# A tuned decoder layer with a product-key expert layer: U blocks, exponential, first loads and LN refinement moved

## The chip, the cores and the metric

The kernel runs on one core of one Trainium2 chip. The metric is the device time of one execution in microseconds (us). A core has five engines that run side by side, each working through its own instructions in order: TensorE (PE; its weight loads are shown apart as PEld), VectorE (DVE), ScalarE (ACT), GpSimd (POOL) and SyncE (SP). SP issues most DMAs, ACT and POOL some. An engine that waits for a semaphore holds up all that stands behind the waiting instruction on it.

## The reference

One inference step of one layer for a prompt of 512 tokens and 8 sequences of 4 tokens, 544 tokens in all, of width 1024. A mixer (pooling and mLSTM, a gated linear recurrence with matrix memory) is followed by PEER, a feed-forward layer that picks 16 of 16384 one-neuron experts for each token and each of 8 heads:

```python
x  = ln(ALPHA * x + (1 + g1) * mixer(ln(x) * (1 + s1) + b1), ln1_g, ln1_b)
u2 = ln(x) * (1 + s2) + b2
q  = (u2 @ w_q).reshape(n, 8, 2, 128)              # two half keys per head
s  = einsum('nhpc,hpkc->nhpk', q, keys)            # scores against 128 sub keys
sv, si = top_k(s, 16)
comb = sv[:, :, 0, :, None] + sv[:, :, 1, None, :]  # 16 x 16 sums
top, sel = top_k(comb, 16); eidx = the experts' numbers (128 * i + j)
g   = softmax(top)
act = gelu(einsum('nd,nhkd->nhk', u2, u_tab[eidx]))
y   = einsum('nhk,nhkd->nd', g * act, v_tab[eidx])
x   = ln(ALPHA * x + (1 + g2) * y, ln2_g, ln2_b)
```

All is float32. u_tab and v_tab have 16384 rows of 1024.

## The kernel before, in words

Float32 products are made from split operands: a weight tile is copied by ACT to a rounded high half (whi, L439), the rest is the low half (wlo, L441, on POOL or DVE), and PE adds three products (high by high, high by low, low by high), 24 matmuls for a 128-row block of w_q or u_tab. The class Weights loads (L414, from SP), splits and hands out these tiles in program order.

**Stages.** Modulation, the first LN, the q, k, v projections and mLSTM come first. Then the out projection: for each of five token tiles (four of 128, one of 32) the LN steps of x1_of run on DVE, POOL and ACT, PE transposes the normalised rows (L160), and u2 and its halves are made. Each LN takes its reciprocal root from ACT and refines it in ln_newton with four DVE instructions of one element per partition (L233 to L239). `halves(0)` is interleaved: the q projection and scores of one half of the tokens.

**halves(1).** The q projection of the other half: 16 steps (hp, head and half key) of 24 matmuls, transposes and scores on PE. ACT copies the scores (L1136), DVE sorts the top 16 (L1102 to L1107) and then the best 16 sums (L1112 to L1116). After the steps listed in PRE, one *U block* (`uphase`, L1174) is put on PE: u_tab rows 128 b to 128 b + 127 against the 384 tokens of the three dense tiles, 24 matmuls into a PSUM bank, then Gelu on ACT (act, L1188); the first SPILL acts are stored to DRAM (Ad, L1190), the last RING stay in SBUF. Every expert of a block is computed for these tokens, so nothing has to be gathered for them.

**Ranks and gates.** `softmax_and_ranks` subtracts the maximum (L1235), takes the exponential on ACT (L1236, with a load of its table, and one for Gelu afterwards), finds each expert's i and j on DVE (L1239 to L1250) and sums and inverts (L1252, L1253). `topk(t)` turns them into numbers and gates g for each tile. The gates of the three dense tiles become a dense array: one-hot masks E (L1318) and P (L1346, E times the gate) on DVE, their products on PE (tile pg, 16 matmuls a group, 24 pairs of two groups), copied by ACT to stage (L1333) and stored to DRAM as Gd in twelve pieces (L1337, ACT's queue).

**The planner.** L1371 to L1392 is a loop at build time with two modelled clocks, pe and dve, the constants GRP, LOU, PEU, PEG, TOFF, LEAD, PEW and a bound GB of groups in flight. It decides whether a DVE step of the side chain (ranks, topk, masks), a pair of gates or a U block comes next. RES blocks are kept for after the last gate; AHEAD = 56 blocks are done before the stream.

**The stream.** From L1588 on, 128 iterations b: a U block (from the iteration on at which todo_u - b is at most RING), then `vprep(b + 2)`, then `ymm(b)`: 18 matmuls (Y) for each of three tiles, coefficients times v rows. vprep (L1476) multiplies act by gate (ar*gr, L1481), splits the loaded v rows (vr; whi on ACT, wlo on DVE) and splits the product (chi on ACT L1484, clo L1485). SP issues the loads: vr (L1459), every fourth time gr from Gd (L1462), and spilled acts ar from Ad (L1470) through the queue object `aq` (class Ahead). The remaining tokens (one prompt tile and the samples) take *gather steps*: POOL gathers rows of u_tab or v_tab by index (L1421), DVE multiplies and sums (L1434 for u, L1446 for v into y); `pace` spreads 320 of them over the iterations. vr and raw share one pool tag of NRAW = 4 buffers.

**The tail.** `finish(t)` per tile: y plus the residual (L1549, L1550), moments (L1558, L1560, L1563), `ln_newton`, scale and shift (ACT L1581, POOL L1582 and L1583), store.

## Time and profile before

| what | value |
|---|---|
| runs, us | 1667.96, 1670.13, 1671.59 (median 1670.13) |
| profiled execution, us | 1665.72, its span 1663.9 |
| busy share of the span | PE 94%, DVE 82%, POOL 43%, ACT 38% |
| mean granted TensorE clock | 0.971 |
| DMA | 455.33 MB, mean 274 GB/s |
| chain that ended last | PE 72%, DVE 16%, DMA 6%, ACT 2%, issue 2% |

The span is the time from the first to the last instruction in the profile; the profiled execution's own time is 1.8 us longer. Stages in it: out projection from about 270 to 423 us, halves(1) to 524, ranks to the first gate at 615, gates to 758, the last U blocks to 787.5, the stream to about 1624, then the tail. Busy time says how long an engine had an instruction running, not whether another waited for it; the waits and the chain say that. The granted clock is a share of TensorE's full clock of 2.4 GHz.

### The profile page before, as it was taken

The numbers are of one execution on the slowest core, as the hardware profiler recorded it, in microseconds if no ns is written. First come the engines' busy times: TensorE is split into PE (matmuls) and PEld (weight loads), VectorE is DVE, ScalarE is ACT, GpSimd is POOL, SyncE is SP. The second block draws the span as 40 slices with busy tenths as digits, with TensorE's granted clock in tenths as the row PEclk, the third lists the DMA queues.
The fourth block names the chain that finished last, engine by engine and source line by source line (L and its number), as shares of the span: only waits on it lengthen the run. The fifth ranks groups of instructions, "written<-read, shape, count | busy, mean of one in ns | idle before, by whom it ended". The sixth has DMA issues, their size and how long they took to land.

```text
span 1663.9 us, 25206 instructions
## 1 busy us (share of the span) xinstructions
PE 1559.0 (94%) x9293; PEld 1386.5 (83%) x9293; DVE 1356.1 (82%) x2734; ACT 632.9 (38%) x999; POOL 712.4 (43%) x521
## 2 busy tenths in 40 slices
PE   5999999896998999999899999999999999999993
PEld 3888777676897999999788889999999999999873
DVE  6634467698996999993688879989999999998986
ACT  4322223445433335554333333333333333333343
POOL 2333333465554000000433336656666666666615
PEclk9999998898999999999899999999999999999997
DMA  8544456443343558876999989999999999999981
GB/s 340 175 145 159 142 148 215 163 165 118 114 142 101 162 163 303 285 274 228 359 364 382 372 297 373 373 371 386 379 372 381 377 371 385 378 369 378 390 281 67
DMA packets 181135, 455.33 MB, mean 274 GB/s; under 512 B 23248, under 2 KB 84304, under 8 KB 179348
## 3 DMA queue, kind: packets, MB, share of 16 engines
q1 hardware_dynamic: 119880, 246.90, 43.3%
q0 software_dynamic: 46080, 167.79, 26.3%
q10 hardware_dynamic: 15052, 39.03, 6.6%
q8 instruction: 73, 1.20, 0.3%
q14 instruction: 50, 0.41, 0.1%
HBM read 412.93 MB, written 40.73 MB: 273 GB/s over the span
## 4 chain that ended last, share of the span: by engine, by line
PE 72%; DVE 16%; DMA 6%; ACT 2%; issue 2%; POOL 1%; SPq 0%; ACTq 0%; DVEq 0%; POOLq 0%
PE pH L156 27%; PE Y L156 25%; PE bk L156 11%; PE tb L156 4%; DMA gr<-Gd 4%; PE pg L156 3%; DVE wlo L441 2%; PE pm L156 1%; DMA wm<-in_w_mod_r_dram 1%; PE tb L160 1%; DVE or L235 1%; DVE y L1446 1%; DVE ost L245 1%; DVE x L979 1%; ACT whi L439 1%
## 5 line engine op out<-in xcount | busy, mean ns | idle before, releaser
L156 PE MATMUL pH<-u2hi,whi 128*128 128x384 f32 x960 | 328.9, 343 | 7.9 <-ACT act L1188 7.9
L156 PE MATMUL pH<-u2hi,wlo 128*128 128x384 f32 x960 | 324.0, 338 | 2.9 <-DVE wlo L441 2.6
L156 PE MATMUL pH<-u2lo,whi 128*128 128x384 f32 x960 | 324.4, 338 | 0.0
L156 PE MATMUL Y<-whi,chi 128*128 128x512 f32 x768 | 301.1, 392 | 8.4 <-ACT chi L1484 8.4
L156 PE MATMUL Y<-whi,clo 128*128 128x512 f32 x768 | 302.6, 394 | 2.2 <-DVE clo L1485 1.5
L1421 POOL DMA_INDIRECT rbuf<-in_v_tab_dram,eid x160 | 237.9, 1487 | 151.8 <-DVE y L1446 104.6
L156 PE MATMUL Y<-wlo,chi 128*128 128x512 f32 x768 | 302.0, 393 | 0.0
L1421 POOL DMA_INDIRECT rbuf<-in_u_tab_dram,eid x160 | 218.4, 1365 | 187.4 <-DVE rbuf L1434 143.2
L439 ACT ACTIVATE whi<-raw 128x1024 fp32r<-128x1024 f32 (+1 forms) x193 | 203.0, 1055 | 200.9 <-issue 126.0
L439 ACT ACTIVATE whi<-vr 128x1024 fp32r<-128x1024 f32 x128 | 135.7, 1060 | 280.6 <-PE Y L156 226.9
L441 POOL TENSOR_TENSOR wlo<-raw,whi 128x1024 fp32r<-128x1024 f32 (+2 forms) x68 | 159.9, 2359 | 181.4 <-ACT whi L439 180.0
L441 DVE TENSOR_TENSOR wlo<-vr,whi 128x1024 fp32r<-128x1024 f32 x128 | 156.5, 1222 | 68.3 <-ACT whi L439 56.7
L1446 DVE SCALAR_TENSOR_TENSOR y<-rbuf,cf,y 128x1024 f32<-128x1024 f32 x158 | 202.6, 1282 | 0.9
L156 PEld LDWEIGHTS pH<-u2hi,whi 128*128 128x128 f32 x960 | 181.0, 189 | 11.2 <-ACT act L1188 8.2
L441 DVE TENSOR_TENSOR wlo<-raw,whi 128x1024 fp32r<-128x1024 f32 (+1 forms) x129 | 155.3, 1207 | 36.9 <-ACT whi L439 34.1
L156 PEld LDWEIGHTS pH<-u2hi,wlo 128*128 128x128 f32 x960 | 180.9, 188 | 5.0 <-DVE wlo L441 4.3
L156 PEld LDWEIGHTS pH<-u2lo,whi 128*128 128x128 f32 x960 | 181.1, 189 | 2.8
L156 PEld LDWEIGHTS Y<-whi,chi 128*128 128x128 f32 x768 | 145.4, 189 | 40.4 <-ACT chi L1484 10.0
L156 PEld LDWEIGHTS Y<-whi,clo 128*128 128x128 f32 x768 | 145.1, 189 | 33.4 <-DVE clo L1485 3.3
L156 PEld LDWEIGHTS Y<-wlo,chi 128*128 128x128 f32 x768 | 145.1, 189 | 30.1
L1434 DVE SCALAR_TENSOR_TENSOR rbuf<-rbuf,utok 128x1024 f32<-128x1024 f32 x128 | 156.1, 1221 | 0.0
L1485 POOL TENSOR_TENSOR clo<-ar,chi 128x384 fp32r<-128x384 f32 x1 | 1.4, 1357 | 250.1 <-DMA ar<-Ad 250.1
(402 smaller groups left out, 2693.5 us busy)
## 6 DMA issues: line engine op xcount, KB each, us to landing
raw<-in_u_b_dram SPq DMA_DIRECT2D x128, 512.0 KB
vr<-in_v_tab_dram SPq DMA_DIRECT2D x128, 512.0 KB
wm<-in_w_mod_r_dram SPq DMA_DIRECT2D x48, 512.0 KB
gr<-Gd SPq DMA_DIRECT2D x32, 768.0 KB
Gd<-stage ACTq DMA_DIRECT2D x9, 2048.0 KB
raw<-in_w_q_b_dram SPq DMA_DIRECT2D x32, 512.0 KB
raw<-in_w_in_b_dram SPq DMA_DIRECT2D x20, 512.0 KB
Ad<-act ACTq DMA_DIRECT2D x43, 192.0 KB
```

What stands on the lines that cost most here:

```text
L156: nc.tensor.matmul(out, l, r, start=start, stop=stop, skip_group_check=True)
L160: nc.tensor.transpose(out, x, idn)
L235: nc.vector.tensor_tensor(r, r, q, op=ALU.mult)
L245: nc.vector.bn_stats(st[:, i, :], x[:, 512 * i:512 * (i + 1)])
L439: nc.scalar.activation(hi, raw, AF.Copy)
L441: e.tensor_tensor(lo[:, d], raw[:, d], f32(hi[:, d]), op=ALU.subtract)
L979: e.tensor_tensor(x1[:, d], x1[:, d], l1b[:rows, d], op=ALU.add)
L1421: nc.gpsimd.indirect_dma_start(out=g, out_offset=None, in_=tab, in_offset=bass.IndirectOffsetOnAxis(ap=eid[t][:, k:k + 1], axis=0))
L1434: nc.vector.scalar_tensor_tensor(g, g, 1.0, u, op0=ALU.mult, op1=ALU.mult, accum_out=dots[:, k:k + 1])
L1446: nc.vector.scalar_tensor_tensor(y2[t], g, cf[:, k:k + 1], y2[t], op0=ALU.mult, op1=ALU.add)
L1485: (nc.vector if b else nc.gpsimd).tensor_tensor(cl, x, f32(ch), op=ALU.subtract)
```

## The change

Constants: PRE has four entries for eight, at steps 4, 7, 10 and 13; AHEAD is 53 for 56, so SPILL 40 for 43; TOFF 10 for 0. ln_newton's three instructions with two tensors become tensor_scalar instructions whose second and third operands are one-element columns read by pointer; the fourth instruction stays. The ranks' function is cut in three: `ranks`, `exps` (issued by the planner's chain after the ranks have been handed out) and `sums` (after the second half of the first topk). The planner's loop ends with the last gate; the blocks left up to AHEAD then stand in a loop of their own, with the loads of spilled acts ahead of them (`aq.fill()`), the first gr when five are left, two gather steps at each of the last three, and vprep(0) and vprep(1) at the last two. WI.early = 2 makes a tile's split go out two calls ahead rather than one, in the planner's loop and until that point.

```diff
-AHEAD = 56
+AHEAD = 53
+GPRE = 2
-TOFF = 0.00
+TOFF = 10.00
-PRE = (6, 8, 10, 11, 12, 13, 14, 15)
+PRE = (4, 7, 10, 13)
...
-        nc.vector.scalar_tensor_tensor(q, r, ve, r, op0=ALU.mult, op1=ALU.mult)
+        nc.vector.tensor_scalar(q, ve, r, r, op0=ALU.mult, op1=ALU.mult)
         nc.vector.tensor_scalar(q, q, -0.5, 1.5, op0=ALU.mult, op1=ALU.add)
-        nc.vector.tensor_tensor(r, r, q, op=ALU.mult)
+        nc.vector.tensor_scalar(r, r, q, None, op0=ALU.mult)
...
-        nc.vector.scalar_tensor_tensor(nm, mv[:, 0:1], sign, r, op0=ALU.mult, op1=ALU.mult)
+        nc.vector.tensor_scalar(nm, mv[:, 0:1], sign, r, op0=ALU.mult, op1=ALU.mult)
...
     def topks():
-        r = softmax_and_ranks()
-        yield 9.0
+        r = ranks()
+        yield 8.5
+        exps(r[0])
...
-            yield 3.7
+            if t == TORD[0] and p:
+                sums(ex, sx)
+            yield 4.2 if K == 128 else 1.6
...
-    while more or wait or b < AHEAD:
+    while more or wait:
...
-        elif b < (AHEAD - RES if more or wait else AHEAD) and not (wait and wait[0][0] <= pe + PEW):
+        elif b < AHEAD - RES and not (wait and wait[0][0] <= pe + PEW):
+            WI.early = 2
...
+    def load_g(b):
+        g = vp.tile([128, 12, 4, 32], F32, name="gr", tag="gr", bufs=2)
+        nc.sync.dma_start(g, Gd[:, :, b:b + 4, :].rearrange("q j i n -> j q i n"))
+        for i in range(4):
+            gpair[b + i] = g
...
-        if b % 4 == 0:
...
+        if b % 4 == 0 and b:
+            load_g(b)
...
-    for b in range(2):
-        vprep(b)
-    todo_u = AHEAD
-    spent, done = 0.0, 0
-    pace = (320 + 1 - GV * (AHEAD - RING) - GV2 * (RING - GEND)) / (NB - AHEAD)
+    todo_u = b
+    aq.fill()
+    while todo_u < AHEAD:
+        if AHEAD - todo_u == 5:
+            load_g(0)
+        if AHEAD - todo_u < 4:
+            steps(gg, GPRE)
+        if AHEAD - todo_u < 3:
+            WI.early = 1
+            vprep(2 - AHEAD + todo_u)
+        uphase(todo_u)
+        todo_u += 1
+    done = 3 * GPRE
+    spent = float(done)
+    pace = (320 + 1 - done - GV * (AHEAD - RING) - GV2 * (RING - GEND)) / (NB - AHEAD)
```

In the order of PE's work, before: eight U blocks in halves(1), then 18 with three sets of transposes among them, then 24 pairs of gates with U blocks between them, the last gate behind block U49, then seven more blocks and the stream with 43 iterations without and then 72 with a U block. In the changed kernel: four, then 19, then the gates, the last behind block U46 (the 47th), six more, and 40 and 75 iterations. The matmuls are the same in number.

ACT at the end of halves(1), before: the copies of the last scores, the exponential's table and the exponential, and behind it the split of a U weight (whi) and the Gelu of a U block (act).

```order
L1136 ACTIVATE scr<-tb 128x256
L1215 ACTIVATE scr<-pm 128x512
L1236 ACT_TABLE_LOAD
L1236 ACTIVATE ex<-ex 128x544
L439 ACTIVATE whi<-raw 128x1024
L1188 ACT_TABLE_LOAD
L1188 ACTIVATE act<-pH 128x384
L1190 DMA Ad<-act 128x384
```

In the changed kernel the exponential stands behind four pairs of whi and act, of which the last two are shown:

```order
L443 ACTIVATE whi<-raw 128x1024
L1192 ACTIVATE act<-pH 128x384
L1194 DMA Ad<-act 128x384
L443 ACTIVATE whi<-raw 128x1024
L1192 ACTIVATE act<-pH 128x384
L1194 DMA Ad<-act 128x384
L1258 ACT_TABLE_LOAD
L1258 ACTIVATE ex<-ex 128x544
L443 ACTIVATE whi<-raw 128x1024
L1192 ACT_TABLE_LOAD
L1192 ACTIVATE act<-pH 128x384
L1194 DMA Ad<-act 128x384
```

What moved: four U blocks' whi, act and store went ahead of the exponential.

DVE behind the sort (L1104, in the changed kernel L1108), before: the ranks run on to the sums, then a split of U weights.

```order
L1241 TENSOR_SCALAR rtmp<-sel 128x544
L1242 CAST rtmp<-rtmp 128x544
L1245 SCALAR_TENSOR_TENSOR rtmp<-rtmp 128x544
L1246 TENSOR_SCALAR rtmp<-rtmp 128x544
L1247 TENSOR_TENSOR ii<-rtmp 128x544
L1248 TENSOR_TENSOR rtmp<-rtmp 128x544
L1249 TENSOR_SCALAR rtmp<-rtmp 128x544
L1250 TENSOR_TENSOR jj<-rtmp 128x544
L1252 TENSOR_REDUCE sx_5728<-ex 128x34
L1253 RECIPROCAL sx_5728<-sx_5728 128x34
L441 TENSOR_TENSOR wlo<-raw,whi 128x1024
```

In the changed kernel a split (wlo of block 7) stands ahead of the ranks, and directly behind jj stand two splits and the first topk; the sums come behind its second half.

```order
L445 TENSOR_TENSOR wlo<-raw,whi 128x1024
L1239 TENSOR_TENSOR ex<-top 128x544
L1242 TENSOR_SCALAR rtmp<-sel 128x544
L1243 CAST rtmp<-rtmp 128x544
L1244 TENSOR_SCALAR rtmp<-sel 128x544
L1245 CAST rtmp<-rtmp 128x544
L1248 SCALAR_TENSOR_TENSOR rtmp<-rtmp 128x544
L1249 TENSOR_SCALAR rtmp<-rtmp 128x544
L1250 TENSOR_TENSOR ii<-rtmp 128x544
L1251 TENSOR_TENSOR rtmp<-rtmp 128x544
L1252 TENSOR_SCALAR rtmp<-rtmp 128x544
L1253 TENSOR_TENSOR jj<-rtmp 128x544
```

What moved: one split ahead of the ranks, the two steps of the sums (the reduction and the reciprocal) behind the first topk.

SP at the stream's first loads, before (raw are U weights, vr v rows, ar spilled acts, gr gates):

```order
L414 DMA raw<-in_u_b_dram 128x1024 x52
L1459 DMA vr<-in_v_tab_dram 128x1024
L1462 DMA gr<-Gd 128x12x128
L1459 DMA vr<-in_v_tab_dram 128x1024 x2
L1470 DMA ar<-Ad 128x384 x5
L1459 DMA vr<-in_v_tab_dram 128x1024
L1470 DMA ar<-Ad 128x384
L1459 DMA vr<-in_v_tab_dram 128x1024
L1462 DMA gr<-Gd 128x12x128
```

In the changed kernel:

```order
L418 DMA raw<-in_u_b_dram 128x1024 x47
L1485 DMA ar<-Ad 128x384 x5
L418 DMA raw<-in_u_b_dram 128x1024
L1471 DMA gr<-Gd 128x12x128
L418 DMA raw<-in_u_b_dram 128x1024 x3
L1477 DMA vr<-in_v_tab_dram 128x1024 x4
L1485 DMA ar<-Ad 128x384
L418 DMA raw<-in_u_b_dram 128x1024
L1477 DMA vr<-in_v_tab_dram 128x1024
L1471 DMA gr<-Gd 128x12x128
```

What moved: the five ar loads and the first gr went ahead of the last U weights and of all vr.

## Rows read from the trace of the kernel before

**Rows 1.** This is the page: the span, the busy time of each engine (share of the span, instructions), and one line of the costliest groups (line, engine, operation, out<-in, count | busy us, mean ns of one | idle time before it).

```profile
span 1663.9 us, 25206 instructions
...
PE 1559.0 (94%) x9293; PEld 1386.5 (83%) x9293; DVE 1356.1 (82%) x2734; ACT 632.9 (38%) x999; POOL 712.4 (43%) x521
...
L441 DVE TENSOR_TENSOR wlo<-raw,whi 128x1024 fp32r<-128x1024 f32 (+1 forms) x129 | 155.3, 1207 | 36.9 <-ACT whi L439 34.1
```

**Rows 2.** This is the table of windows, whole program by stage. Columns: window, its length in us, busy us and number of instructions of PE, of PE's weight loads, of DVE, of ACT and of POOL, granted TensorE clock (1 is full), DMA share, GB/s.

```profile
300.00:423.00 123.00, 94.06 (x653) 80.60 (x651) 101.79 (x331) 61.51 (x121) 69.17 (x43) 0.86 0.44 147
524.00:603.00 79.00, 68.24 (x371) 65.67 (x370) 76.86 (x191) 26.85 (x35) 2.92 (x1) 0.94 0.40 128
603.00:758.00 155.00, 155.00 (x1392) 151.22 (x1392) 145.85 (x179) 87.80 (x147) 0.00 (x0) 1.00 0.78 271
758.00:787.50 29.50, 29.47 (x168) 29.15 (x166) 8.57 (x7) 10.35 (x15) 0.00 (x0) 1.00 0.64 208
787.50:820.30 32.80, 25.61 (x90) 19.92 (x91) 18.21 (x26) 9.44 (x13) 13.81 (x13) 0.84 0.97 357
820.30:960.00 139.70, 139.70 (x618) 115.65 (x617) 119.58 (x169) 52.61 (x70) 48.13 (x42) 1.00 1.03 372
960.00:970.00 10.00, 7.37 (x32) 5.54 (x31) 5.68 (x9) 2.24 (x4) 1.21 (x2) 1.00 0.71 260
1000.00:1570.00 570.00, 570.00 (x2872) 518.90 (x2871) 517.50 (x652) 202.39 (x282) 369.24 (x248) 1.00 1.01 378
```

**Rows 3.** These are waits of PE from 355 to 423 us: line that waited <- engine and line that ended the wait: us in total, times, longest.

```profile
PE tb L160 <- ACT xh L988: 9.7, 2, 5.0
PE bk L156 <- POOL wlo L441: 8.3, 2, 4.6
PE tb L156 <- POOL ut L1012: 2.8, 1, 2.8
```

**Rows 4.** This is the timeline of DVE, POOL and PE between 373 and 419 us, picked rows in order of time. Columns: start, duration in us (of all, where several are joined), engine, line, operation, out<-in, shapes, count, in brackets the idle time before and what ended it.

```profile
373.56 1.26 POOL L942 TENSOR_TENSOR es<-es,G1s 32x512 f32<-32x512 f32 x1
...
373.73 3.41 DVE L235 TENSOR_TENSOR or<-or,oq 128x1 f32<-128x1 f32 x1
...
391.14 4.78 POOL L441 TENSOR_TENSOR wlo<-raw,whi 128x1024 fp32r<-128x1024 f32 x2 [0.51 <-ACT whi L439]
...
391.51 2.08 DVE L235 TENSOR_TENSOR or<-or,oq 32x1 f32<-32x1 f32 x1
...
393.62 2.31 DVE L239 SCALAR_TENSOR_TENSOR onm<-omv,or 32x1 f32<-32x1 f32 x1
...
411.55 2.09 DVE L235 TENSOR_TENSOR or<-or,oq 32x1 f32<-32x1 f32 x1
...
418.97 1.30 PE L156 MATMUL tb<-con,ut 128*32 128x128 f32 x20 [2.85 <-POOL ut L1012]
```

**Rows 5.** These are two lines of source over the whole span: engine, operation, count: shortest, median and longest duration in ns, first and last start, shapes.

```profile
L234 DVE TENSOR_SCALAR oq<-oq x16: 142/154/155, 289.8 to 1656.7; 128x1 f32<-128x1 f32 x13, 32x1 f32<-32x1 f32 x3
...
L1558 DVE TENSOR_SCALAR omv<-fsu x4: 202/214/215, 1607.1 to 1642.9; 128x1 f32<-128x1 f32 x3, 32x1 f32<-32x1 f32 x1
```

**Rows 6.** This is the timeline of DVE at 124 us, while POOL ran a weight split from 124.40 for 2.35 us.

```profile
124.31 2.55 DVE L643 TENSOR_SCALAR hs<-sx,hmv,hr 32x128 f32<-32x128 f32 x1
```

**Rows 7.** These are waits of PE from 523 to 603 us.

```profile
PE pH L156 <- ACT act L1188: 7.9, 1, 7.9
PE pH L156 <- DVE wlo L441: 2.6, 4, 1.2
```

**Rows 8.** These are waits of DVE from 423 to 536 us.

```profile
DVE scr L1102 <- ACT scr L1136: 15.0, 5, 6.0
```

**Rows 9.** This is the timeline of ACT and DVE between 536 and 611 us: the exponential, the last step of the ranks, the first masks P.

```profile
536.53 0.66 ACT L1236 ACTIVATE ex<-ex 128x544 f32<-128x544 f32 x1 [10.67 <-DVE ex L1235]
...
543.64 1.14 DVE L1250 TENSOR_TENSOR jj<-rtmp 128x544 f16<-128x544 f32 x1
...
609.40 1.28 DVE L1346 TENSOR_TENSOR P<-E,gp 128x1024 f16<-128x1024 f16 x2
```

**Rows 10.** These are two pieces of the chain of waits, in order of time: start, us, what (engine, tile, line, number of matmuls): the gates of two groups, and a U block.

```profile
615.31 1.85 PE pg L156 x32
617.16 4.27 PE pH L156 x24
```

**Rows 11.** These are waits of PE from 787 to 1000 us.

```profile
PE Y L156 <- ACT chi L1484: 8.2, 3, 3.8
PE Y L156 <- DVE clo L1485: 1.0, 2, 0.5
```

**Rows 12.** This is the timeline of ACT's and SP's queues (ACTq and SPq issue DMAs; the time is that of issuing, waits for buffers among it) and of DVE, 758 to 813 us.

```profile
758.67 0.81 ACTq L1337 DMA_DIRECT2D Gd<-stage  x2
...
786.40 2.32 SPq L1470 DMA_DIRECT2D ar<-Ad  x5
...
794.58 0.43 SPq L1462 DMA_DIRECT2D gr<-Gd  x1
...
812.55 0.56 DVE L1481 TENSOR_TENSOR ar<-ar,gr 128x384 f32<-128x384 f32 x1 [5.46 <-DMA gr<-Gd]
```

**Rows 13.** This is the timeline of DVE in the tail: the first and the last of three such rows.

```profile
1631.51 1.15 DVE L235 TENSOR_TENSOR or<-or,oq 32x1 f32<-32x1 f32 x1
...
1645.49 1.03 DVE L235 TENSOR_TENSOR or<-or,oq 128x1 f32<-128x1 f32 x1
```

More of the change, by code (lines that the diff above doesn't have):

```diff
@@ L131, in __init__, with fill @@
         self.issue, self.n, self.depth, self.q, self.k = issue, n, depth, [], 0
-    def get(self):
+    def fill(self):
         while self.k < self.n and len(self.q) < self.depth:
@@ L136, in get @@
             self.k += 1
+    def get(self):
+        self.fill()
         r = self.q.pop(0)
@@ L1228, in body, with ranks @@
     heads_of = [slice(8 * t, 8 * t + 8) for t in range(4)] + [slice(32, 34)]
-    def softmax_and_ranks():
+    def ranks():
         ex = grl.tile([128, HS, 16], F32, name="ex")
@@ L1235, in softmax_and_ranks @@
         nc.vector.tensor_tensor(ex, top, top[:, :, 0:1].to_broadcast([128, HS, 16]), op=ALU.subtract)
-        nc.scalar.activation(ex, ex, AF.Exp)
         hk = "q h k -> q k h"
@@ L1251, in softmax_and_ranks, with exps, sums @@
         sx = grl.tile([128, HS], F32, name="sx2")
+        return ex, sx, ii, jj
+    def exps(ex):
+        nc.scalar.activation(ex, ex, AF.Exp)
+    def sums(ex, sx):
         nc.vector.tensor_reduce(sx, ex, op=ALU.add, axis=AX.X)
         nc.vector.reciprocal(sx, sx)
-        return ex, sx, ii, jj
     def topk(t, ex, sx, ii, jj):
@@ L1459, in load_v @@
         nc.sync.dma_start(r, a["v_tab"][128 * b:128 * (b + 1), :])
-        if b % 4 == 0:
-            g = vp.tile([128, 12, 4, 32], F32, name="gr", tag="gr", bufs=2)
-            nc.sync.dma_start(g, Gd[:, :, b:b + 4, :].rearrange("q j i n -> j q i n"))
-            for i in range(4):
-                gpair[b + i] = g
+        if b % 4 == 0 and b:
+            load_g(b)
         return r
```

## The prediction

> **What bounds the kernel now.** I read the page first: PE is busy 94% of a span of 1663.9 us, VectorE (DVE) 82% [rows 1]. So a gain can only come from stretches in which PE stands or runs at a lower clock, and the table of windows by stage finds them [rows 2]. From 1000 to 1570 PE is busy 570.00 of 570 us at a granted clock of 1.00, likewise 603 to 758 and 820.3 to 960: there a change only shifts. PE loses time in five places: 300 to 423 (94 of 123 busy, clock 0.86), 524 to 603 (68 of 79), 787.5 to 820.3 (25.6 of 32.8, clock 0.84), 960 to 970 and the tail. The change touches all five. For each I read PE's waits with their releasers, then the timeline of the engine named, back to its first late instruction. After the last gate the order of PE's work is fixed, so what PE gains in one of these places stays gained, unless a later wait has another cause.
>
> **Part 1, refinement by pointer scalars (LN steps of the out projection).** PE's waits there are for the transposes' input (L988), for POOL's low half of the weights and for ut: 20.8 us together [rows 3]. The DVE timeline shows what is late before them: one-element two-tensor operations that take about 0.2 us elsewhere take 3.41, 2.08, 2.31 and 2.09 us [rows 4], and each ends with a POOL tensor_tensor that ran meanwhile (the pair of weight splits at 391.14, 4.78 us, covers the two at 391.51 and 393.62) [rows 4]. The new form has one tensor input and its scalars by pointer. The kernel has that form at one place, L1558: 202 to 215 ns over four executions, three of which overlap a POOL tensor_tensor [rows 5]. L234, one element with immediate scalars, is 142 to 155 ns sixteen times [rows 5]. So I take 0.2 us per new instruction, some 0.05 more than an undisturbed old one.
> What is late next: at 373.73 the following operation, with two tensors of 32x512, waits for POOL's es (373.56 + 1.26) [rows 4] and then meets the same POOL split: 0.85 of 3.2 us gained. At 391 the refinement ends about 4 us sooner, but a two-tensor sorting step behind it meets the second split; the row of x reaches POOL 3.1 us earlier, and PE, which waits there for POOL's split [rows 3], resumes as much earlier. The second refinement, with 409.75 to 413.8, then needs 0.8 us and no POOL work runs beside it: PE resumes at 413.4 instead of 418.97 [rows 4]. I take **-5.6 us**; bounds -2 (only the 3.1 with one more stall) and -8 (every excess of the four rows counted once, 1.8 + 2.1 + 1.9 + 2.2).
> The Trainium skill ("SBUF — State Buffer", Who interferes with whom) says that a DVE instruction with two SBUF inputs contends with a GpSimd one that reads SBUF, and one with at most one doesn't outside the two-port modes: [rows 4] and the L234 and L1558 lines of [rows 5] agree. It also says that tensor_scalar can enter those modes and is then blocked. The trace has that too: L643, a tensor_scalar with two pointers on 128 elements, takes 2.55 us [rows 6]. By the first rule the sum is -5.6, by the second 0: that is rival 1.
>
> **Part 2, four U blocks between the projections, and the exponential behind the ranks.** Before, 371 matmuls in 524 to 603 at 4.27 us per 24 [rows 2, 10] would need 66.0 of 79 us: 13.0 lost. The waits are 7.9 for ACT's act at L1188 and 2.6 for DVE's splits [rows 7], the rest clock (0.94). ACT stands 10.67 us on the exponential, until DVE has sorted [rows 9], with the act copies queued behind it. In the new order four whi and act pairs stand ahead of it: that wait goes.
> What is late next is DVE. It waits 15.0 us in 423 to 536 for scores [rows 8]. Four U blocks fewer let PE end its projections 4 x 4.27 = 17 us earlier, at 506.4 in the old frame (523.4 less 17); the sort can only gain its 15.0 idle us. It ended at about 535.8 (the subtraction, 0.7 us, ends with the exponential's start at 536.53, [rows 9]); I add 0.7 for the last scores: 521.5. PE does U4 to U6, whose splits are POOL's, until 519.2, then stands for wlo(7), one DVE split of 1.2 us [rows 1] behind the sort: U7 from 522.7 to 527. wlo(8) stands behind the ranks (535.8 to 544.7, 8.9 us [rows 9]): U8 starts at 532.8, ends at 537.1. Lost: 3.5 + 5.8 = 9.3. The remaining 14 blocks take 59.8 and the transposes 1: first gate at 597.9, or up to 602.5 with the clock and split waits that before also showed. DVE's first P comes 74.8 us behind its ranks (535.8 to 610.7, [rows 9]), plus one split more: 597.5, just in time. Before, the first gate ran at 615.31 [rows 10] behind three U blocks more, so break-even is 615.3 - 12.8 = 602.5. Gain 0 to 4.6; I take **-2 us**, below the middle since the three waits add up, with a bound of +5 if DVE's queue, not PE, sets the first gate. Gates stay PE's: 4.27 + 1.85 us per pair [rows 10], and every such slot before was gapless.
>
> **Part 3, first loads between the last U blocks.** Before, 90 matmuls in 787.5 to 820.3 at 139.7/618 = 0.226 us [rows 2] need 20.3 of 32.8: 12.5 lost, in PE's waits for chi and clo and in the clock of 0.84 [rows 2, 11]. The chain back: chi waits for DVE's ar*gr, that for the spilled ar, which SP issues only at 786.40 behind vr loads that wait for buffers; gr(4), issued at 794.58, is still waited for at 812.55 [rows 12]. Meanwhile DMA moves 208 GB/s from 758 to 787.5 and 357 after [rows 2]: 29.5 us with 149 GB/s to spare are 4.4 MB, which at 357 are 12.3 us. So the stretch can take what the start lacks. In the new order the five ar loads go out at the last gate, gr(0) behind the gates' store, v rows and six gather steps beside U47 to U52 (6 x 4.27 = 25.6 us). The new costs: gr(0) waits for the store (last part issued at 758.67, about 1 us behind the last gate, [rows 12]); behind it on SP stand the weights of the last U blocks and vr. With some 8 us for 2 MB it goes out at 9 and lands at 13 to 27 us (18 us was the crowded case of gr(4)); needed at about 20. So 0 to 8.4 us are lost; I take 2.5: **-10 us**, range -4 to -12.5. The six gather products that go ahead of the splits on DVE fit where it is busy 8.57 of 29.5 us [rows 2]. Steps done early lower the pace of steps in the U stretch, where PE is full anyway: 0. The wait at 965 (2.6 lost in ten, [rows 2]) has the same cause, a gr behind others; three fewer iterations without U and six steps less behind them: **-1** (0 to -3).
>
> **Part 4, tail.** Three refinements, at 1631.51 to 1645.49, have one stalled step each, 1.15 to 1.03 us [rows 13], on the chain that ends the kernel; at 0.2 each they give 2.6, and the next operation reads PSUM. **-2.5** (-1 to -2.6).
>
> Sum: -5.6 - 2 - 10 - 1 - 2.5 = -21.1. The profiled execution took 1665.72 (span 1663.9 and 1.8 around it): 1644.6. The median of the runs is 4.4 above that execution, so on its scale **1649 us**.
>
> **Rivals.** Rival 1: the pointer form stalls like L643. Then parts 1 and 4 give nothing, -13: 1657. For it, L643; against, three L1558 rows beside POOL at 0.2 us. Rival 2: DVE takes the place of ACT in part 2: the sort doesn't come 15 us earlier, as its idle time was not all PE's. With S unmoved U7 starts at 537, 17.7 us idle, and U8 5.8: 26 with the clock against 13, so +13 in place of -2: 1664; halfway 1656. For it, DVE at 76.9 of 79 busy; against, every idle piece before names a score. Rival 3, slower: the head of SP's queue. gr(0) waits there for the store, with the last weights and all vr behind. If the store shares 208 GB/s with ar, one weight tile and four gathers (2 + 1 + 0.5 + 2 MB by their shapes), it ends 26 us behind the last gate, gr lands 18 us later, the first Y runs at 48 instead of 25.6: 22.4 lost and about 4.5 of low clock, 27 against 12.5. With the others' -11.1: +3.4, **1673.5**. It decides from a loss of 23.6. For it, gr(4)'s 18 us; against, 357 GB/s as soon as loads are there. Rival 4: the loads come early but DMA, at its limit until 960, hands the loss on to the iterations behind: part 3 near 0 and a new wait; with part 2 at +5 that makes about -3: 1667, no change.
>
> **Numbers.** Forecast case 0.62, own range 1643 to 1656 (parts 1 to 4 at most -31, at least about -14); rival 1 0.10; rival 2 0.15, of it 0.02 no faster; rival 3 0.08; rival 4 0.05. A measurement of this kernel tells about 0.2% (3.3 us) from no change. Faster by more: 0.62 + 0.10 + 0.13 = 0.85; within it 0.07; slower 0.08. The range takes in rivals 1 and 2: 1640 to 1664.
>
> **What would show it.** Part 1: L235 and L239's successors at 0.2 us beside POOL's splits, PE's transposes about 5 us earlier. Part 2: act no longer behind the exponential, PE's longest wait in that stretch for a DVE split of about 6 us, the first gate 13 to 17 us before 615.3 beside the front's shift. Part 3: Y at 0.226 us from its first iteration, DMA above 300 GB/s between last gate and first Y, gr(0) landing within 20 us of the last gate. Part 4: tail 2.5 us shorter. It is wrong if the new one-element steps still show 2 us, if PE waits over 12 us for DVE behind the projections, or if Y's first matmul comes over 10 us behind the last U block.

## The result and the profile after

The changed kernel takes 1655.42 us (median of ten runs, 1650.67 to 1667.01); the kernel before, on the same chip, 1671.30. The ratio is 0.9908, with an interval of 0.9879 to 0.9938: about 15 us faster, 10 to 20. On a second chip (a run below) the ratio was 0.9940, 0.9918 to 0.9962. The profiled execution took 1654.74, its span is 1653.0: 10.9 under the span shown of before. The forecast was 1649, the range 1640 to 1664.

Lines of the changed kernel are numbered 4 higher than before up to the ranks and 8 or more higher behind them. One thing is to be put right in the section on the change: WI.early counts the weight tiles loaded ahead of their split, so with 2 the load, not the split, goes out earlier.

The table of windows of the changed kernel by stage, with columns as in [rows 2]:

```profile
417.00:501.00 84.00, 84.00 (x581) 78.89 (x581) 83.25 (x553) 38.19 (x61) 48.01 (x20) 1.00 0.42 131
501.00:594.50 93.50, 84.17 (x466) 82.21 (x466) 87.60 (x229) 33.18 (x43) 2.40 (x1) 0.98 0.44 146
594.50:743.00 148.50, 148.48 (x1346) 144.70 (x1346) 138.08 (x165) 84.75 (x144) 2.16 (x2) 0.99 0.73 264
743.00:769.40 26.40, 25.75 (x144) 24.80 (x142) 9.95 (x13) 6.43 (x10) 10.63 (x8) 1.00 1.00 377
769.40:800.00 30.60, 26.50 (x102) 20.85 (x103) 23.59 (x33) 13.18 (x18) 11.92 (x9) 0.89 1.02 376
```

The projections before, from the same view of the kernel before:

```profile
423.00:524.00 101.00, 101.00 (x677) 95.90 (x676) 85.73 (x570) 43.90 (x70) 57.43 (x24) 1.00 0.44 136
```

To be read against [rows 2]: the stretch behind the projections is 501 to 594.5 and loses 9.3 us (84.17 of 93.50) where it lost 10.8; DVE, 85.7 of 101 before in the projections, is now busy 83.25 of 84.00 in them. Between last gate and first Y (743 to 769.4) DMA moves 377 GB/s, not 208. From 769.4 to 800 PE is still short, 26.50 of 30.60 at a clock of 0.89.

PE's waits in the changed kernel, in three stretches: 355 to 417 us (against [rows 3]), 501 to 600 ([rows 7]) and 769 to 1000 ([rows 11]):

```profile
PE bk L160 <- POOL wlo L445: 6.1, 3, 3.3
PE tb L164 <- ACT xh L992: 5.9, 3, 4.1
PE tb L160 <- POOL ut L1016: 3.5, 1, 3.5
...
PE pH L160 <- DVE wlo L445: 6.5, 4, 3.4
PE pg L160 <- DVE P L1356: 2.7, 1, 2.7
...
PE Y L160 <- ACT chi L1499: 3.6, 3, 1.9
PE Y L160 <- POOL clo L1500: 1.1, 1, 1.1
PE Y L160 <- DVE clo L1500: 1.0, 2, 0.5
```

The wait for act behind the exponential (7.9 us) is gone; in its place stand DVE's splits and its first mask P, 9.2 us together. The waits between 769 and 1000 us are 5.7 us together, where those of before were 9.2 and 0.6 more for POOL's clo; Y begins 1.9 us behind the last U block. DVE's wait for scores from 417 to 517 us (15.0 us in [rows 8]) is down to one of 0.4:

```profile
DVE scr L1106 <- ACT scr L1140: 0.4, 1, 0.4
```

The refinement's last two instructions over the whole span, as two lines of source (against [rows 5]):

```profile
L239 DVE TENSOR_SCALAR or<-or,oq x16: 201/214/216, 291.3 to 1646.3; 128x1 f32<-128x1 f32 x13, 32x1 f32<-32x1 f32 x3
...
L243 DVE TENSOR_SCALAR onm<-omv,or x15: 200/215/217, 291.6 to 1646.5; 128x1 f32<-128x1 f32 x12, 32x1 f32<-32x1 f32 x3
```

And the timeline of POOL and DVE where a split ran beside them (against [rows 4]):

```profile
390.76 2.38 POOL L445 TENSOR_TENSOR wlo<-raw,whi 128x1024 fp32r<-128x1024 f32 x1 [0.50 <-ACT whi L443]
...
391.19 0.20 DVE L239 TENSOR_SCALAR or<-or,oq 32x1 f32<-32x1 f32 x1
391.43 0.20 DVE L243 TENSOR_SCALAR onm<-omv,or 32x1 f32<-32x1 f32 x1
```

The longest of 31 is 217 ns; at 391.19 and 391.43 both run inside POOL's split from 390.76 to 393.14, where before one took 2.08 and the other 2.31.

**Where the time went.** Every stage, in us, for all kernels that ran, from one profiled execution each: A is from the first matmul of the q projections on u2 to the first transpose of the last tile's ut, B from there to the start of the ranks on DVE, C from there to the first gate, D to the last gate, E from there to the end of the stream's last U block, F to the last Y, G to the end.

| kernel | A | B | C | D | E | F | G | span | ratio to before |
|---|---|---|---|---|---|---|---|---|---|
| before | 91.1 | 116.8 | 79.4 | 142.8 | 816.7 | 65.0 | 24.3 | 1663.9 |  |
| changed | 84.6 | 103.2 | 77.8 | 148.4 | 820.6 | 67.5 | 22.0 | 1653.0 | 0.9908 |
| changed, again | 86.9 | 103.7 | 76.5 | 147.0 | 821.7 | 67.1 | 21.9 | 1655.7 | 0.9940 |
| before with the refinement | 84.9 | 117.9 | 79.3 | 142.8 | 816.9 | 66.2 | 22.2 | 1657.2 | 0.9959 |
| two columns | 91.7 | 103.7 | 76.5 | 147.0 | 822.0 | 66.9 | 25.3 | 1664.2 | 1.0010 |
| exponential ahead | 84.7 | 110.2 | 76.5 | 148.6 | 822.9 | 67.7 | 21.9 | 1663.4 | 0.9919 |
| start undone | 85.4 | 104.4 | 76.4 | 147.0 | 827.9 | 67.0 | 22.0 | 1657.7 | 0.9946 |
| no steps ahead | 84.2 | 103.7 | 76.5 | 147.0 | 820.8 | 66.6 | 21.9 | 1649.9 | 0.9927 |
| gathers four deep | 85.1 | 110.0 | 76.5 | 148.6 | 827.1 | 66.8 | 22.0 | 1661.3 | 0.9958 |
| chi first | 85.2 | 110.0 | 76.5 | 148.6 | 817.7 | 67.6 | 21.9 | 1660.2 | 0.9922 |
| chi first, gr(4) early | 84.8 | 110.1 | 76.5 | 148.6 | 826.8 | 67.2 | 21.9 | 1662.6 | 0.9977 |
| splits in two | 80.1 | 104.1 | 76.5 | 147.0 | 820.8 | 67.9 | 22.3 | 1648.4 | 0.9918 |
| all three | 81.0 | 103.8 | 77.7 | 148.6 | 831.0 | 67.7 | 22.3 | 1660.7 | 0.9922 |
| splits in two, chi first | 78.0 | 103.4 | 77.7 | 148.4 | 819.0 | 66.4 | 22.3 | 1641.4 | 0.9871 |

Before has 79 U blocks in E, the changed kernels 81; so 816.7 is to be compared as 816.7 + 2 x 4.27 = 825.3. D holds one block more than before (147.0 for 142.8 + 4.27). Before's first gate stands behind 26 U blocks, the changed kernel's behind 23: 12.8 us of PE work. The stretch ahead of A is not in the table: it is 325 to 333 us (327.9 before, 329.0 in the changed kernel), and why it differs wasn't tried.

### The profile page after: what moved, and what is told of

It reads as the page before. It is cut to its first block, busy times and chain, and to the rows that moved or that the text cites. A ratio compares the mean times of both kernels' runs of the same rounds, so it can differ in the third digit from the quotient of the medians.

```text
span 1653.0 us, 25192 instructions
## 1 busy us (share of the span) xinstructions
PE 1560.3 (94%) x9293; PEld 1385.3 (84%) x9293; DVE 1349.8 (82%) x2738; ACT 630.5 (38%) x999; POOL 702.0 (42%) x517
## 4 chain that ended last, share of the span: by engine, by line
PE 74%; DVE 13%; DMA 5%; issue 3%; ACT 2%; POOL 2%; SPq 0%; ACTq 0%; POOLq 0%; DVEq 0%
PE Y L160 27%; PE pH L160 27%; PE bk L160 10%; PE tb L160 4%; PE pg L160 3%; DMA gr<-Gd 2%; PE pm L160 1%; DVE wlo L445 1%; DMA wm<-in_w_mod_r_dram 1%; POOL wlo L445 1%; DMA raw<-in_u_b_dram 1%; PE tb L164 1%; DVE i L1108 1%; DVE scr L1106 1%; DVE scr L1111 1%
## 5 line engine op out<-in xcount | busy, mean ns | idle before, releaser
L1433 POOL DMA_INDIRECT rbuf<-in_u_tab_dram,eid x160 | 211.9, 1324 | 421.8 <-DMA ar<-Ad 235.3
L160 PE MATMUL pH<-u2hi,wlo 128*128 128x384 f32 x992 | 334.8, 338 | 6.9 <-DVE wlo L445 6.8
L160 PE MATMUL pH<-u2hi,whi 128*128 128x384 f32 x992 | 339.8, 343 | 0.4 <-ACT act L1192 0.4
L160 PE MATMUL pH<-u2lo,whi 128*128 128x384 f32 x992 | 335.1, 338 | 0.0
L1433 POOL DMA_INDIRECT rbuf<-in_v_tab_dram,eid x160 | 244.5, 1528 | 188.7 <-DVE y L1458 133.2
L445 DVE TENSOR_TENSOR wlo<-vr,whi 128x1024 fp32r<-128x1024 f32 x128 | 156.7, 1224 | 91.7 <-ACT whi L443 87.9
L445 POOL TENSOR_TENSOR wlo<-raw,whi 128x1024 fp32r<-128x1024 f32 (+2 forms) x64 | 149.7, 2348 | 156.7 <-ACT whi L443 155.3
L160 PEld LDWEIGHTS pH<-u2hi,wlo 128*128 128x128 f32 x992 | 186.9, 188 | 8.9 <-DVE wlo L445 8.9
L445 DVE TENSOR_TENSOR wlo<-raw,whi 128x1024 fp32r<-128x1024 f32 (+1 forms) x133 | 161.9, 1220 | 37.4 <-ACT whi L443 37.2
L160 PEld LDWEIGHTS pH<-u2hi,whi 128*128 128x128 f32 x992 | 187.2, 189 | 3.8 <-ACT act L1192 0.7
L1192 ACT ACTIVATE act<-pH 128x384 f32<-128x384 f32 x124 | 59.4, 479 | 111.1 <-PE pH L160 111.1
```

Source lines behind the costliest of these rows:

```text
L160: nc.tensor.matmul(out, l, r, start=start, stop=stop, skip_group_check=True)
L445: e.tensor_tensor(lo[:, d], raw[:, d], f32(hi[:, d]), op=ALU.subtract)
L1192: nc.scalar.activation(x, p[:, 0:ND], AF.Gelu)
L1433: nc.gpsimd.indirect_dma_start(out=g, out_offset=None, in_=tab, in_offset=bass.IndirectOffsetOnAxis(ap=eid[t][:, k:k + 1], axis=0))
```

## The experiments

**The refinement alone, put into the kernel before.**

```diff
-        nc.vector.scalar_tensor_tensor(q, r, ve, r, op0=ALU.mult, op1=ALU.mult)
+        nc.vector.tensor_scalar(q, ve, r, r, op0=ALU.mult, op1=ALU.mult)
...
-        nc.vector.tensor_tensor(r, r, q, op=ALU.mult)
+        nc.vector.tensor_scalar(r, r, q, None, op0=ALU.mult)
...
-        nc.vector.scalar_tensor_tensor(nm, mv[:, 0:1], sign, r, op0=ALU.mult, op1=ALU.mult)
+        nc.vector.tensor_scalar(nm, mv[:, 0:1], sign, r, op0=ALU.mult, op1=ALU.mult)
```

> The kernel before with the pointer-scalar refinement alone. Theory A (the one-element two-tensor steps stood behind POOL's tensor_tensor work, and the wait doesn't come back elsewhere): the transposes of the last out-projection tile come 5 to 6 us earlier, the tail is 2.3 us shorter, the time 7 to 9 us under the kernel before. Rival B (the stall passes to the next two-tensor operation on DVE): under 3 us in the front, and the time 2 to 4 us under before.

Measured: 1662.73 against 1670.11, ratio 0.9959 (0.9941 to 0.9977), 7 us. Stage A falls from 91.1 to 84.9, G from 24.3 to 22.2; B and F are 1.1 and 1.2 longer, the rest as before. Theory A holds.

**Two columns in place of one.** The same instructions, three of the four on two columns in place of one (the first's input repeated); the expectation below counts two, but the second step went along with the first.

```diff
+        q2 = sm.tile([128, 2], F32, name="oq", tag="oq")[:rows]
+        q = q2[:, 0:1]
-        nc.vector.tensor_scalar(q, ve, r, r, op0=ALU.mult, op1=ALU.mult)
-        nc.vector.tensor_scalar(q, q, -0.5, 1.5, op0=ALU.mult, op1=ALU.add)
+        nc.vector.tensor_scalar(q2, ve.to_broadcast([rows, 2]), r, r, op0=ALU.mult, op1=ALU.mult)
+        nc.vector.tensor_scalar(q2, q2, -0.5, 1.5, op0=ALU.mult, op1=ALU.add)
...
-        nm = sm.tile([128, 1], F32, name="onm", tag="onm")[:rows]
-        nc.vector.tensor_scalar(nm, mv[:, 0:1], sign, r, op0=ALU.mult, op1=ALU.mult)
+        nm = sm.tile([128, 2], F32, name="onm", tag="onm")[:rows]
+        nc.vector.tensor_scalar(nm, mv[:, 0:2], sign, r, op0=ALU.mult, op1=ALU.mult)
...
```

> The changed kernel with two of the four refinement steps (L238 and the last) on two columns instead of one, the second column unused. Theory A (a tensor_scalar on an even number of float32 columns in SBUF can go two elements at a time and then stands behind POOL): these steps take 1 to 2.4 us wherever a POOL tensor_tensor runs (about 374, 391 and three places in the tail), and 3 to 7 us of the gain go. Rival B (a tensor_scalar with pointer scalars this small never stands behind POOL): 0.14 to 0.22 us everywhere, time that of the changed kernel within 1.5 us.

Measured: 1669.80, ratio 1.0010 (0.9988 to 1.0032): the whole gain of the change is gone. Two lines of source (shortest, median, longest in ns):

```profile
L239 DVE TENSOR_SCALAR oq<-oq x16: 168/170/2311, 291.2 to 1657.3; 128x2 f32<-128x2 f32 x13, 32x2 f32<-32x2 f32 x3
...
L244 DVE TENSOR_SCALAR onm<-omv,or x15: 216/228/3357, 291.6 to 1657.8; 128x2 f32<-128x2 f32 x12, 32x2 f32<-32x2 f32 x3
```

The timeline of DVE and POOL from 376 us on:

```profile
376.66 1.27 POOL L947 TENSOR_TENSOR es<-es,G1s 32x512 f32<-32x512 f32 x1
...
376.90 3.36 DVE L244 TENSOR_SCALAR onm<-omv,or 128x2 f32<-128x2 f32 x1
...
377.90 2.33 POOL L446 TENSOR_TENSOR wlo<-raw,whi 128x1024 fp32r<-128x1024 f32 x1
```

The median of the last step rises by 13 ns, its longest to 3.36 us: it lasts until POOL's L947 and the split behind it are done (380.23). Stage A is 91.7, as before the change, and G 25.3: 10.4 us more in these two than in the changed kernel (8.2 against its second execution), above the 3 to 7 of theory A. The third step (L240), which stayed on one column, takes at most 0.215 us in the same kernel. So the pointer form alone isn't what helps: a tensor_scalar on two float32 columns stands behind POOL as a two-tensor instruction does, one on a single column doesn't. What was left out of the forecast's sum as rival 1 is real, one column away.

**The stream's start undone.**

```diff
-        if b % 4 == 0 and b:
+        if b % 4 == 0:
...
-    aq.fill()
     while todo_u < AHEAD:
-        if AHEAD - todo_u == 5:
-            load_g(0)
-        if AHEAD - todo_u < 4:
-            steps(gg, GPRE)
         if AHEAD - todo_u < 3:
             WI.early = 1
-            vprep(2 - AHEAD + todo_u)
         uphase(todo_u)
         todo_u += 1
-    done = 3 * GPRE
+    for i in range(2):
+        vprep(i)
+    done = 0
```

> The changed kernel with the stream's first loads, first gr and vprep(0), vprep(1) behind the last U block again, and no gather steps ahead. Theory A: the early loads are worth the 5 to 6 us by which the stretch from the last U block to the full rate of Y is shorter than before, so this kernel is 4 to 7 us over the changed one. Rival B (DMA is at its limit from the last gate to 940 us, so whatever is loaded early is paid for later): within 2 us of the changed kernel, with a longer wait in front of the first Y and a shorter one 70 us behind it.

Measured: 1660.27, ratio 0.9946 (0.9919 to 0.9972), which lies so near the changed kernel's 0.9908 and 0.9940 that the time alone doesn't decide. The stage does: E is 827.9, 6 to 7 us longer, with waits at 770.09 (3.9 and 0.8) and 795.18 (4.65) as before the change had (3.8 and 0.6, then 2.3 and 0.5). Theory A by the stage: the early loads are worth 6 to 7 us there. That E is also 2.6 longer than the 825.3 of before: something else in the change costs about that much there, and what wasn't tried.

**Where the rest of the start goes.** Three kernels and the changed one again, on one chip. First, no gather steps ahead (GPRE = 0):

> The changed kernel without the six gather steps between the last U blocks, so that POOL's first gather goes out behind the first clo. Theory A (from the last gate on DMA is full, and the ten gathers of 0.5 MB take 5 MB, 13 us at 377 GB/s, from the weights of the last blocks and the first v rows): the weights issued behind the ar loads land 4 to 6 us sooner, Y starts with no wait and at full clock, and the stretch from the last gate to the stream's last U block is 2 to 5 us shorter than the 820.6 of the changed kernel; some of it comes back as a wait for gr or vr when the burst follows. Rival B (the burst costs the same wherever it stands): the stretch within 2 us of 820.6.

Measured: 1656.36, ratio 0.9927 (0.9901 to 0.9954); the changed kernel again 1659.95, 0.9940. E is 820.8: no shorter. The first Y now follows the last U block without a wait and at full clock, and 23 us later PE waits 6.3 us, which hangs on this row of DVE:

```profile
787.34 0.56 DVE L1496 TENSOR_TENSOR ar<-ar,gr 128x384 f32<-128x384 f32 x1 [9.43 <-DMA gr<-Gd]
```

Rival B holds: DMA's share is 0.82 from the last gate to the first Y (740.6 to 765.75), where it was 1.00, and 1.03 in the 34 us behind it; the burst of gathers costs the same wherever it stands. Second, gathers four ahead instead of seven:

> The changed kernel with gathers at most four ahead of their use in place of seven. Theory A of the run without steps ahead: seven instead of ten gathers in front of the first clo, 1.5 MB or 4 us of DMA less: the first vr lands 2 to 4 us sooner, the stretch from the last gate to the stream's last U block 1 to 4 us shorter. Rival B: four ahead are too few for a gather's time, DVE waits for gathers, and the stretch is as long or up to 5 us longer.

Measured: 1661.87, ratio 0.9958 (0.9935 to 0.9982), E 827.1, 5 to 7 us longer, so theory A is wrong. PE waits 6.7 us for a product that stood 9.8 us for gr(4); DMA falls to 262 GB/s in the 14 us from the last U block ahead of Y on and is full again in the next 20. Rival B has the number but not the cause: DVE waits for no gather. So too many gathers at a time isn't the fault; put later, they fall on gr(4). Third, the order on ACT and DVE:

```diff
+        if b < 2:
+            nc.scalar.activation(ch, x, AF.Copy)
+            nc.vector.tensor_tensor(cl, x, f32(ch), op=ALU.subtract)
         hi, lo = split(raw, [128, D], ON_DVE, vp if b >= NB - XB else None)
-        nc.scalar.activation(ch, x, AF.Copy)
-        (nc.vector if b else nc.gpsimd).tensor_tensor(cl, x, f32(ch), op=ALU.subtract)
+        if b >= 2:
+            nc.scalar.activation(ch, x, AF.Copy)
+            nc.vector.tensor_tensor(cl, x, f32(ch), op=ALU.subtract)
```

> The changed kernel with chi and clo of the first two iterations ahead of the split of their v rows, and the first clo on DVE. Theory C (PE's waits of 1.9 and 1.1 us at the first Y are ACT's and POOL's queue order, the product being there 3 us before): both waits under 0.6 us, Y at full clock from its start, and 3 to 6 us shorter from the last gate to the last U block. Theory A (the first v rows land too late anyway): the wait at Y stays 1 us or more, now for the split of the v rows, gain under 2 us.

In the changed kernel the product ar*gr was there at 767.67, and chi stood behind the split of v rows that landed 2.1 us later; timeline of DVE, ACT and PE:

```profile
767.11 0.56 DVE L1496 TENSOR_TENSOR ar<-ar,gr 128x384 f32<-128x384 f32 x1
...
769.78 1.06 ACT L443 ACTIVATE whi<-vr 128x1024 fp32r<-128x1024 f32 x1 [5.76 <-DMA vr<-in_v_tab_dram]
770.74 0.51 ACT L1499 ACTIVATE chi<-ar 128x384 fp32r<-128x384 f32 x1
...
771.30 0.59 PE L160 MATMUL Y<-whi,chi 128*128 128x512 f32 x1 [1.92 <-ACT chi L1499]
```

Measured: 1656.03, ratio 0.9922 (0.9897 to 0.9947), not to be told from the changed kernel's 0.9940 by the time; E 817.7, 3 to 4 us shorter (the kernels that leave this stretch as it is have 820.6 to 822.9, the last one below, which has chi first too, 819.0). The wait at the first Y is still 1.72, for the v rows' split, as theory A said, and the rest of the gain is theory C's: clo no longer waits and the clock falls less (0.88 in the 14 us from the first Y on and 1.00 in the next 20, where the changed kernel had 0.76 and, in its two executions, 1.00 and 0.91).

> The changed kernel as it is, on the chip of the three runs above, for comparison: ratio to before 0.988 to 0.994, the stretch from the last gate to the last U block 819 to 823 us.

Measured: ratio 0.9940 and E 821.7, as expected.

Then gr(4) ahead of the v rows, with chi first:

```diff
-        if b % 4 == 0 and b:
+        if b % 4 == 0 and b > 4:
...
             WI.early = 1
+            if AHEAD - todo_u == 2:
+                load_g(4)
             vprep(2 - AHEAD + todo_u)
```

> The kernel with chi and clo of the first two iterations ahead of the split of their v rows, and gr(4) besides issued ahead of the first v rows in place of behind them. The stretch from the last gate to the stream's last U block was 820.6 and 821.7 us in the changed kernel and 817.7 with chi first. Theory A (DMA is full there: whatever is put ahead, something else lands later): 816 to 819, no wait for gr(4), but 2 us more in front of the first Y. Rival B (gr(4)'s place in SP's queue was a cost of its own): 814 to 816.

Measured: 1666.65, ratio 0.9977 (0.9954 to 1.0000), E 826.8: 9 us longer than with chi first alone, where the two theories had 1.3 more at most. Rows of SP's queue and of PE:

```profile
762.23 0.52 SPq L1471 DMA_DIRECT2D gr<-Gd  x1
765.81 22.12 SPq L1477 DMA_DIRECT2D vr<-in_v_tab_dram  x4
...
785.24 0.79 PE L160 MATMUL Y<-whi,chi 128*128 128x512 f32 x1 [9.52 <-ACT whi L443]
```

Behind gr(4) the first v rows, issued at 765.81, are split from 784.1 on, 18 us later and not 9 (761.02 to 769.78 in the changed kernel). gr(4) itself took 20.6 us to land, and the issue of the first v rows 8.9 us on SP, where it takes 0.3 in the changed kernel. A load of gr is 0.79 MB, 2 us at 377 GB/s; put ahead of the v rows it made the first Y wait 8 us more than with chi first alone (9.52 for 1.72). In the trace gr goes in packets of 512 bytes and the v rows in packets of 4096; that this is the cause is likely, not shown.

**The exponential ahead of the acts.**

```diff
         nc.vector.tensor_tensor(ex, top, top[:, :, 0:1].to_broadcast([128, HS, 16]), op=ALU.subtract)
+        nc.scalar.activation(ex, ex, AF.Exp)
...
         yield 8.5
-        exps(r[0])
```

> The changed kernel with the exponential directly behind the subtraction, ahead of the acts of U blocks 4 to 7, as before. Theory A (with four blocks less between the projections DVE sets the first gate, so PE's waits ahead of it only change places): PE waits some 9 us for act instead of 2.6 and 3.4 us for splits, the wait for the first mask P of 2.7 us goes, first gate and time within 2 us of the changed kernel. Rival B (the wait behind the exponential comes on top): first gate and time 4 to 8 us later.

It is issued ahead of two of the four acts, not of all, as the planner puts two blocks in front. Measured: 1657.58, ratio 0.9919 (0.9887 to 0.9952), not to be told from the changed kernel; but its profiled execution is 5.7 us longer from the last score to the first gate. That looked like rival B until the kernel with chi first, which leaves the exponential where it was, showed the same waits. PE's waits from 503 to 605 us with the exponential ahead:

```profile
PE pH L160 <- DVE wlo L445: 11.4, 4, 9.6
PE pg L160 <- DVE P L1357: 2.7, 1, 2.7
```

And from 505 to 605 us in the kernel with chi first:

```profile
PE pH L160 <- DVE wlo L445: 11.5, 4, 9.6
PE pg L160 <- DVE P L1356: 2.7, 1, 2.7
```

No wait for act came and the wait for P stayed, so theory A's waits were wrong; its time was right. The 5.7 us have another cause, and in this execution the place of the exponential is worth nothing: DVE sets the first gate (C is 76.5 in both).

**What those 7 us are.** Stage B is 103 to 104 us in some executions and 110 in others, of kernels that don't differ there. Here are the sums in front of the best 16 (L1116 to L1120) on DVE and the start of POOL's splits, first the timeline of the changed kernel run again (B 103.7):

```profile
425.25 0.20 DVE L1116 TENSOR_TENSOR scr<-scr 128x32 f32<-128x32 f32 x1
425.34 0.29 DVE L1117 TENSOR_TENSOR scr<-scr 128x112 f32<-128x112 f32 x1
425.53 0.19 DVE L1120 TENSOR_TENSOR scr<-scr 128x16 f32<-128x16 f32 x1
...
425.90 7.14 POOL L445 TENSOR_TENSOR wlo<-raw,whi 128x1024 fp32r<-128x1024 f32 x3 [5.90 <-ACT whi L443]
```

The same place in the kernel with chi first (B 110.0):

```profile
425.35 7.13 POOL L445 TENSOR_TENSOR wlo<-raw,whi 128x1024 fp32r<-128x1024 f32 x3 [5.17 <-ACT whi L443]
...
425.44 2.36 DVE L1116 TENSOR_TENSOR scr<-scr 128x32 f32<-128x32 f32 x1
427.72 2.50 DVE L1117 TENSOR_TENSOR scr<-scr 128x112 f32<-128x112 f32 x1
430.14 2.36 DVE L1120 TENSOR_TENSOR scr<-scr 128x16 f32<-128x16 f32 x1
```

In the first DVE's sums start 0.65 us ahead of three splits of POOL, in the second 0.09 us behind: then each of the three stands behind a split, 7.2 us in place of 0.7, and the sort never makes it up. Later sums stand 1.5 us each in both. All nine profiled executions with four U blocks in the projections and whole splits fall into these two kinds. In five the first of the three sums starts 0.12 to 0.86 us ahead of the first split; the 39 sums of stage B take 16.0 to 16.7 us together, and B is 103 to 104. In four it starts 0.11 us ahead to 0.09 behind, one to three of the three stand 2.3 to 2.5 us, some of the next ones 2.2; the sums take 22.9 to 23.2, and B is 110. The test was to cut POOL's splits in two:

```diff
...
+    IN_TWO = ((nc.gpsimd, slice(0, 4)), (nc.gpsimd, slice(4, 8)))
...
-        jobs.append((a["w_q_b"][hp], 128, ON_POOL))
+        jobs.append((a["w_q_b"][hp], 128, IN_TWO))
```

(the same for the U blocks whose split is POOL's.)

> The changed kernel with POOL's weight splits of w_q and of the first U blocks in two instructions of half the length. Theory D (in halves(1) DVE's sort is now what ends last, and its two-tensor sums of L1116 to L1120 stand behind POOL's splits, 1.5 us eight times and in some executions 7 us more at its start): these stalls fall to 0.8 us or less, the sort ends 10 to 13 us behind the last score in place of 15.7 or 22.7, and the stage from the last score to the first gate takes 87 to 91 us, not 92.2 or 99.2; median 3 to 7 us under the changed kernel. Rival E (PE's and DVE's own work sets that stage; the stalls only fill slack): 92 or 99 us as before, time within 2 us of the changed kernel.

Measured: 1654.44, ratio 0.9918 (0.9891 to 0.9946). Theory D's numbers fail: single sums still stand 1.1 to 1.4 us, B is 104.1 and the stage from the last score to the first gate 92.3. The execution of B 110 didn't occur in three kernels with split instructions; with whole ones it did in the four of nine. In one of the three (the last kernel below) a sum did come 0.03 us behind the first split and stood 1.3 us, not 2.4. That the cut prevents B 110 isn't shown by so few. What gained was a place that theory D didn't speak of: stage A is 80.1 instead of 84.6. There, too, two-tensor steps of the LN and POOL's own steps stand behind splits of 2.4 us; that this is the cause is likely and was not tried by itself.

**Versions that combine.** All three:

> The changed kernel with splits in two instructions, chi first and gr(4) early together. If theory D and the order of the first Y hold, the two gains add: 6 to 10 us under the changed kernel's 1655 to 1660, so 1647 to 1653. If D falls, 1652 to 1657.

Measured: 1655.86, ratio 0.9922 (0.9897 to 0.9946): A 81.0, but E 831.0 (the first Y waits 11.7 us for its v rows); gr(4) early takes back what the rest gives. Without it:

> The changed kernel with POOL's splits in two instructions and chi first, gr(4) left where it was. The front took 80.1 and 81.0 us with splits in two (84.6 without), the stretch from the last gate to the last U block 817.7 with chi first (820.6 and 821.7 without). If the two are independent they add: front 80 to 81, stretch 816 to 819, and a ratio to before of 0.984 to 0.990. If the gain of chi first was that run's luck: stretch 820 to 823 and ratio 0.989 to 0.993.

Measured: 1647.72 (1643.15 to 1653.96), ratio 0.9871 (0.9842 to 0.9900), A 78.0, E 819.0. It beats the kernel before clearly, and the changed one by 0.4 to 0.7% by the ratios (0.9908 and 0.9940, on other chips; the interval of the first still overlaps by 0.002).

## Why the prediction was right

The time, 1655.42, lies in the range of 1640 to 1664 and, by 0.6 us, in the 1643 to 1656 that the forecast gave to its own case (the bounds of its parts, added up, would give 1639 to 1668). The gain is smaller than the sum: 15.9 by the medians and 10.9 by the profiled executions, where the sum had 21.1. The range was drawn to take in two rivals, and that is why it holds a result in which part 3 gave less than half. By the profiled executions, span against span, -10.9:

| step | forecast | measured |
|---|---|---|
| part 1, out projection | -5.6 | -6.5 in A (91.1 to 84.6), of which 1.1 was lost ahead of it |
| part 2, to the first gate | -2 | -2.4 at the first gate (-20.6, less 12.8 of PE work and 5.4 of the front) |
| gates (D) | 0 | +1.3 (0 in the second execution) |
| part 3 and the wait at 965 | -11 | -4.7 (825.3 to 820.6) |
| end of the stream (F) | 0 | +2.5 |
| part 4, tail | -2.5 | -2.3 |

Part 1 and 4 were right in mechanism and size, and the refinement alone shows it: 7 us against 8.1. So most of the gain that these runs can tell comes from the three instructions: alone they have 0.9959 (0.9941 to 0.9977), the whole change 0.9908 (0.9879 to 0.9938) and, again, 0.9940 (0.9918 to 0.9962), which overlaps with theirs. In the bound of -8 one of the four excesses was taken as 2.2; the row of 3.41 us gives 3.2, and the bound would be -9. The weighing of rival 1 by L1558 against L643 was the right comparison, and the run with two columns shows that the number of columns decides between the two rows. The Trainium skill ("SBUF — State Buffer", Who interferes with whom) has both halves of that: two SBUF inputs contend (3.41 and 2.31 us before), a tensor_scalar can contend where it enters a two-port mode (3.36 us on two columns, 0.217 at most for the same step on one). The trace shows the wait, not the mode.

Part 2 came out at its size, with the waits that were named: 2.64 and 3.42 for splits behind the sort and the ranks (forecast 3.5 and 5.8), and 2.7 for P, which the forecast had as just in time. That is in part luck of the execution: the same sum (B and C against before, less 12.8) gives -2.4 to -3.2 in the five executions with B of 103 to 104 and +3.1 to +3.3 in the four with 110, where PE waits 14 us for DVE, more than the 12 that the forecast named as a sign of being wrong. What it left out is that a sort without slack inherits its own stalls: before, DVE had 15.0 us of idle time [rows 8] in which two-tensor sums could stand behind POOL; with 0.4 us left, 7 us more or less of them go straight to the first gate. That is the spread of the runs for at least these profiled ones, and it is rival 2 in a form that the forecast hadn't: not the idle time, but POOL's splits.

Part 3 is the step that failed: forecast -11 with the wait at 965, measured -4.7. "So the stretch can take what the start lacks" counted 149 GB/s of spare DMA against the 12.3 us lost, but not what the change itself put there. The DMA queues from the last gate to the end of the last U block ahead of Y, in the changed kernel (743 to 769.4); a line has packets, MB and the share of the DMA engines, q0 carries the gathers, q1 what SP issues (U weights, v rows, ar and gr):

```profile
q1 hardware_dynamic: 2752, 4.19, 45.6%
q0 software_dynamic: 993, 3.64, 35.8%
```

The same before (758 to 787.5), where q0 has no line:

```profile
q1 hardware_dynamic: 2437, 4.01, 44.3%
```

DMA moves 9.95 MB in place of 6.13, and the gathers (those of the six steps and of up to seven steps ahead of them) are 3.64 of the 3.8 MB more: they took the spare rate, and what SP issued moved 0.2 MB more than before. DMA was full, 377 GB/s, from the last gate on. The weight tile issued at 744.31 landed 13.4 us later, the first v rows 0.4 us behind the last U block, and gr(4), issued at 779.96, was waited for until 791.25. Undoing the early loads costs 6 to 7 us in the stretch, leaving the early gathers out moves the loss by 23 us and doesn't shrink it, an earlier gr(4) costs 9: what these runs point to is a transfer limit, and 3 to 4 us of the loss are the order of chi behind the v rows. This is rival 4, in part: 6 of the 11 us were handed on. Y didn't run at 0.226 us a matmul from its first iteration, as the forecast had it, but at 0.43 until 778 (clock 0.76 in its first 14 us, behind waits of 1.92 and 1.11). The wait at 965 is gone from its place but stands at 843 (1.1 and 0.55). In F, which is 2.5 us longer, PE waits 1.5 and 0.8 us at 1601 for chi and clo, whose product DVE made only at 1598.7, behind gather steps and first steps of the tail and 11 us after it had stood 4.4 us for a gr; the cause wasn't tried.

The median moved by more (15.9) than the profiled executions (10.9). Before's profiled execution was 5.6 us under its median, the changed kernel's 0.7; why stays open, since one profile of before can't tell.

## What to carry to other kernels

Look which engine waits in the stretch that a change shortens: what had slack there loses it, and every small stall that the slack covered (here sums that stand behind another engine's instruction) becomes time, and spread between runs. Before loads are moved into a stretch that looks idle, add up what the moved work itself transfers there; where DMA was full here, later gathers only moved the wait and an earlier gr made it longer, and what helped was to let nothing that was ready stand behind what still had to land. Small per-row steps on one column with pointer scalars never waited for GpSimd in these runs; the same steps on two columns did.
